# Probabilities of the sparse attention transposed by VectorE and moved by DMAs, instead of by TensorE through PSUM

## The chip, the cores and the metric

One core of one Trainium2 chip. The metric is the device time of one execution in microseconds (us); before and after are compared by the median of several runs. The rows shown come from one profiled execution.

## The reference, cut to what matters

A two-layer decoder trunk in float32: 512 tokens, model width 1024, batch 1. Layer 1 is retention with a gated output and a gated per-layer embedding. One projection then gives the keys and values of three attention branches, and a small MLP compresses one of them. Layer 2 is the sparse attention, in which 16 query heads of 4 groups attend to the compressed blocks, to selected blocks and to a window. With 512 tokens there are 8 selection blocks and up to 16 may be chosen, so that the selected branch, like the 512-token window, is plain causal attention here:

```python
s_s = jnp.einsum('bgrqd,bgqnkd->bgrqnk', q, ks).astype(jnp.float32) * scale
p_s = jnp.where(valid_s, jax.nn.softmax(jnp.where(valid_s, s_s, NEG), axis=(-2, -1)), 0.0)
o_s = jnp.einsum('bgrqnk,bgqnkd->bgrqd', p_s, vs.astype(jnp.float32))
...
return gates[..., 0:1] * o_c + gates[..., 1:2] * o_s + gates[..., 2:3] * o_w
```

The merged heads pass a SiLU gate and the output projection; a second gated embedding and a last RMSNorm end the kernel.

## The kernel before

Every float32 product is three matmuls (`mm3`, L355 of the profile) on operands split into a high and a low part: high by high, high by low, low by high. ScalarE makes the high part, VectorE subtracts it to get the low part (`split_psum`, L364 and L365).

**Weights** come as a stream of 128x1024 pieces (`Stream`). `load` (L143) issues the DMAs of pieces on SyncE's queue (SP) into four raw buffers, `mul` (L176, GpSimd) multiplies by the norm's gain, `high` (L190, ScalarE) and `low` (L205, VectorE) split. `W.tick` advances this by a step or two; the order of the pieces is written out in `order`, and a raw buffer is loaded anew once `low` has read it. The schedule is manual: each engine works in program order.

**The attention** has 4 groups `g` of 8 units `u`; a unit is one head `h` (`u // 2`) in one branch `b` (`u % 2`). A pass of the loop over `u` does:

- `scores` of the *next* unit: matmuls in three PSUM banks, mask (L937, L940), row maxima (L944) on VectorE, exponentials with row sums (L945) on ScalarE into `P[u % 2]`, of which there are two. For every second unit it also starts the compressed branch (`cmp_probs`, a generator advanced by `next(chain)`).
- up to four steps of `fillers` (`fill(0)` to `fill(2)`): halves of a gate or query projection (`g_proj`, `q_proj`), or pairs of tiles of the output projection (`pair_tiles`, whose sums VectorE adds at L1006).
- `scale_probs` of the next unit: the reciprocal (L954) and a product (L955) on VectorE, then four multiplications on GpSimd (L958).
- `probs_T` of the *present* unit: its lower triangle has ten 128x128 blocks. TensorE transposes them (L967) into the banks `pt`, eight in part 0 and two in part 1, and each bank is split into `tH` and `tL`.
- `values` of the present unit: the product of `tH`, `tL` with the values, which accumulates in bank `o` over the two branches of a head.

Between groups stand two `k_proj` (before the scores of the next group's unit 0) and four `v_proj` (after the group's last `values`). Group 3 has no projections after it. Before the attention lie the key and value projection (`v_proj` of group 0, from three pieces `kvb`) and the compression (`compress`), whose generators are interleaved with `c_proj` and the four `q_proj` of group 0; in it `block` adds a position vector (L783, VectorE) to gathered tokens and splits the sum (L785, L788).

## Time and profile before

| | |
|---|---|
| median of 3 runs | 1173.96 us (1173.95 to 1174.43) |
| the profiled execution: its own time | 1176.46 us |
| its span in the profile | 1174.7 us |
| granted TensorE clock, mean | 0.988 of full |
| busy: PE (matmul) | 1140.1 us, 97% |
| busy: DVE (VectorE) | 727.8 us, 62% |
| busy: ACT (ScalarE) | 490.8 us, 42% |
| busy: POOL (GpSimd) | 294.9 us, 25% |
| DMA moved | 101.90 MB, mean 87 GB/s |

PE is TensorE's matmul side, PEld its loading of weights, SPq the DMA issue on SyncE's queue. L and a number is a line of the kernel. A busy PE is not necessarily at its peak, since matmuls are pipelined and their ends are modelled: starts are the better measure. An idle time in brackets is that of the engine just before an instruction, with what ended it.

### The profile page before, as it was taken

The page shows a single profiled execution, that of the slowest core. Times are in us where ns is not written, and L with a number is a line of the kernel's source. Part 1 is how long each engine was busy: PE and PEld are TensorE (multiplying, and loading weights), DVE is VectorE, ACT ScalarE, POOL GpSimd, SP SyncE. Part 2 cuts the span into 40 slices and gives each one's busy share as a digit, 9 for nine tenths or more (in the row PEclk, how much of TensorE's full clock was granted, in tenths as well). Part 3 has the DMA queues.
Part 4 walks back from the last instruction along what each step waited for, and adds up shares of the span by engine and source line. Part 5 has one row for each costly group of instructions (what it writes and reads, how often), then busy time and mean ns, then how long its engine had stood idle before and what let it go on. Part 6 is the DMA issues. An engine that isn't in the chain of part 4 may idle for free. (4 is left out here: it accounts for less than half of the span.)

```text
span 1174.7 us, 15278 instructions
## 1 busy us (share of the span) xinstructions
PE 1140.1 (97%) x5806; PEld 970.0 (83%) x5806; DVE 727.8 (62%) x1242; ACT 490.8 (42%) x916; POOL 294.9 (25%) x341
## 2 busy tenths in 40 slices
PE   8999999999999999899699999999999999999997
PEld 7888888888888888888587888888898888887886
DVE  4746336544534556467857764778468774787555
ACT  6333233232323445345446443444344533444653
POOL 0212003002100222223435331454243431321012
PEclk9999999999999999999799999999999999999999
DMA  8422321322232131255512201221121211221211
GB/s 326 141 97 72 111 96 54 93 95 72 90 108 90 54 124 39 83 152 175 149 69 73 73 21 51 73 74 56 50 91 54 73 54 41 86 77 50 72 37 71
DMA packets 29593, 101.90 MB, mean 87 GB/s; under 512 B 3536, under 2 KB 3792, under 8 KB 29520
## 3 DMA queue, kind: packets, MB, share of 16 engines
q1 hardware_dynamic: 29088, 100.15, 26.2%
q8 instruction: 45, 0.74, 0.3%
q10 hardware_dynamic: 432, 0.79, 0.2%
q14 instruction: 28, 0.23, 0.1%
HBM read 98.83 MB, written 2.10 MB: 86 GB/s over the span
## 5 line engine op out<-in xcount | busy, mean ns | idle before, releaser
L355 PE MATMUL d<-arenaR 128*128 128x512 f32 (+2 forms) x2904 | 678.1, 386 | 10.4 <-DVE arenaF L1006 3.6
L355 PEld LDWEIGHTS d<-arenaR 128*128 128x128 f32 x2904 | 525.6, 189 | 113.9 <-DVE arenaF L1006 5.5
L355 PE MATMUL s<-arenaR 128*128 128x512 f32 (+8 forms) x1182 | 239.5, 353 | 0.2 <-DVE arenaR L829 0.2
L205 DVE TENSOR_TENSOR arenaR<-arenaF,arenaR 128x1024 fp32r<-128x1024 f32 (+1 forms) x142 | 194.1, 1386 | 66.1 <-ACT arenaR L190 66.0
L355 PEld LDWEIGHTS s<-arenaR 128*128 128x128 f32 x1182 | 200.3, 188 | 29.8 <-DVE arenaR L829 0.3
L190 ACT ACTIVATE arenaR<-arenaF 128x1024 fp32r<-128x1024 f32 (+1 forms) x142 | 145.8, 1048 | 104.4 <-PE s L355 68.4
L176 POOL TENSOR_TENSOR arenaF<-arenaF 128x512 f32<-128x512 f32 x108 | 137.0, 1291 | 126.2 <-DMA arenaF<-stream_dram 126.1
L355 PE MATMUL o<-arenaR 128*128 128x512 f32 (+3 forms) x744 | 133.4, 331 | 11.0 <-DVE arenaR L788 5.0
L355 PEld LDWEIGHTS o<-arenaR 128*128 128x128 f32 x744 | 119.1, 198 | 24.0 <-DVE arenaR L788 5.8
L958 POOL TENSOR_SCALAR arenaF<-arenaF 128x512 f32<-128x512 f32 (+3 forms) x128 | 66.8, 541 | 254.1 <-ACT arenaR L364 120.1
L945 ACT ACTIVATE arenaF<-s,arenaF 128x512 f32<-128x512 f32 (+3 forms) x128 | 67.6, 528 | 102.9 <-DVE arenaF L944 100.2
L365 DVE TENSOR_TENSOR arenaR<-pt,arenaR 128x512 fp32r<-128x512 f32 (+1 forms) x141 | 82.8, 617 | 35.5 <-ACT arenaR L364 33.8
L364 ACT ACTIVATE arenaR<-pt 128x512 fp32r<-128x512 f32 (+1 forms) x141 | 70.7, 540 | 80.0 <-PE pt L967 40.4
L371 POOL TENSOR_TENSOR arenaF<-arenaF 128x1 f32<-128x1 f32 (+1 forms) x25 | 14.2, 568 | 294.7 <-DVE arenaF L370 294.7
L944 DVE TENSOR_REDUCE arenaF<-s 128x1 f32<-128x512 f32 (+3 forms) x128 | 62.9, 491 | 22.2 <-ACT arenaF L945 18.9
L355 PE MATMUL pt<-arenaR 128*128 128x512 f32 (+1 forms) x384 | 75.9, 349 | 0.0
L355 PEld LDWEIGHTS pt<-arenaR 128*128 128x128 f32 x384 | 62.7, 188 | 9.4
L209 DVE SCALAR_TENSOR_TENSOR arenaR<-arenaF,arenaR 128x512 fp32r<-128x512 f32 x64 | 45.7, 762 | 35.0 <-PE pt L355 21.4
L194 ACT ACTIVATE arenaR<-arenaF 128x512 fp32r<-128x512 f32 x64 | 43.1, 721 | 46.6 <-issue 22.3
L967 PEld LDWEIGHTS pt<-arenaF 128*128 128x128 f32 x318 | 38.4, 141 | 12.1 <-DVE arenaR L365 4.5
L967 PE MATMUL pt<-arenaF 128*128 128x128 f32 x318 | 45.1, 273 | 3.2 <-DVE arenaR L365 3.2
L1006 DVE TENSOR_TENSOR arenaF<-arenaF,d 128x512 f32<-128x512 f32 x64 | 41.8, 682 | 7.0 <-PE d L355 6.7
(126 smaller groups left out, 692.6 us busy)
## 6 DMA issues: line engine op xcount, KB each, us to landing
arenaF<-stream_dram SPq DMA_DIRECT2D x174, 512.0 KB, 3.5
arenaF<-xT_dram SPq DMA_DIRECT2D x8, 256.0 KB, 5.0
arenaF<-x_dram SPq DMA_DIRECT2D x4, 512.0 KB, 8.3
out_dram<-arenaF SPq DMA_DIRECT2D x3, 512.0 KB, 2.6
arenaF<-cst_dram SPq DMA_DIRECT2D x4, 256.0 KB, 3.8
arenaF<-stream_dram ACTq DMA_DIRECT2D x2, 256.0 KB, 4.4
arenaF<-stream_dram SPq DMA_DIRECT2D x2, 256.0 KB, 6.0
arenaF<-cst_dram SPq DMA_DIRECT2D x1, 512.0 KB, 9.9
```

The lines of the kernel that those rows point to most:

```text
L176: self.nc.gpsimd.tensor_mul(r3[:, k], r3[:, k], g[:, k, None].to_broadcast([128, m // 2, w]))
L190: self.nc.scalar.activation(hi[:, :m * w], raw, AF.Copy)
L194: self.nc.scalar.activation(hi[:, c], raw[:, c], AF.Copy, scale=g[:, k:k + 1])
L205: self.nc.vector.tensor_sub(lo[:, :m * w], raw, hi[:, :m * w])
L209: self.nc.vector.scalar_tensor_tensor(lo[:, c], raw[:, c], g[:, k:k + 1], hi[:, c], op0=OP.mult, op1=OP.subtract)
L355: pe.matmul(o, a, b, start=start and i == 0, stop=stop and i == n - 1)
L364: act.activation(h, src, AF.Copy)
L365: dve.tensor_sub(l, src, h.bitcast(F32))
L944: dve.reduce_max(mx[:, i:i + 1], w, axis=mybir.AxisListType.X, negate=True)
L945: act.activation(Pu[:, PO[i]:PO[i] + n], w, AF.Exp, bias=mx[:, i:i + 1], accum_out=sm_[:, i:i + 1])
L958: pool.tensor_scalar(w, w, sm_[:, i:i + 1], 1.0, op0=OP.mult, op1=OP.mult)
L967: pe.transpose(p[:, f:f + 128], Pu[:, PO[i] + 128 * j:PO[i] + 128 * j + 128], ident)
```

## The change

- `probs_T` now serves the *next* unit. VectorE transposes 32x32 blocks inside each group of 32 partitions, four instructions that write `pt1`; then 16 DMAs on SyncE's queue, each of 32 partitions by 320 float32 (40 KB), move the squares between the groups of partitions into `pt2`. There is one `P`, one `pt1` and one `pt2`.
- `probs_split` (new) makes `tH` and `tL` of the present unit from `pt2` with one ScalarE and one VectorE instruction of 128x1280, both from SBUF. It stands after the scores of the next unit and ahead of `fill(0)` and `scale_probs`. `values` reads `tH` and `tL` in runs of 32 elements.
- `probs_T` stands after `fill(1)`, ahead of `W.tick`; that of the first unit before the loop.
- Beside it: `block` adds the position on GpSimd; the stream's order and the loop over `q_proj` put the last two compression pieces around the fourth `q_proj`; the first `v_proj` are cut in two (`v_sums`), so that the products with the first two of the three pieces of three token tiles come before those with the third.

```diff
     for n, dense in (("wk", [("kv", 0, 1024, 512 + 128 * g, 128) for g in range(4)]),
-                     ("wv", q(0)[:3])):
+                     ("wv", q(0))):
         o += [("w2", 0, 512, 0, 128)] if n == "wv" else []
         for i, d in enumerate(dense):
             o += [d] + [(n, 512 * (2 * i + e), 512, 0, 256) for e in (0, 1)]
-    o += [("wv", 512 * i, 512, 0, 256) for i in (6, 7)] + [q(0)[3]] + kk(0)
+    o += kk(0)
...
-    P = [V(fb + 4096 + 1280 * i, 1280) for i in range(2)]
+    g2 = [V(fb + o, 512) for o in (1664, 7680)]
+    P = V(fb, 1664)
+    pt1, pt2 = V(fb + 2176, 1280), V(fb + 3456, 1280)
...
-    def v_proj(g, t, p, bank="d", tick=True):
-        n = 256 if g else 304
-        o = psum(bank)[:, :n]
-        k0 = 0
+    def v_sums(t, o, p, k0):
         for q in p:
             m = q.h.shape[1]
             mm3(o, [(aH[:, t, k0 + k], aL[:, t, k0 + k], q.h[:, k], q.l[:, k])
                     for k in range(m)], k0 == 0, k0 + m == NK)
             k0 += m
+    def v_proj(g, t, p, bank="d", tick=True, o=None):
+        if o is None:
+            o = psum(bank)[:, :256]
+            v_sums(t, o, p, 0)
+        else:
+            v_sums(t, o, p[2:], 6)
...
-            dve.tensor_add(B[:, :, :, :31], src,
-                           pos[:, :, None, None].to_broadcast([128, 4, 4, 31]))
+            pool.tensor_add(B[:, :, :, :31], src,
+                            pos[:, :, None, None].to_broadcast([128, 4, 4, 31]))
...
-    v_proj(0, 0, p, "d", False)
-    v_proj(0, 1, p, "o", False)
+    o = [psum(bank)[:, :304] for bank in ("d", "o", "d", "s")]
+    v_sums(0, o[0], p[:2], 0)
+    v_sums(1, o[1], p[:2], 0)
     to_aT(3, hn[1])
-    v_proj(0, 2, p, "d", False)
+    v_sums(2, o[2], p[:2], 0)
+    v_proj(0, 0, p, tick=False, o=o[0])
+    v_proj(0, 1, p, tick=False, o=o[1])
     W.tick(1)
-    v_proj(0, 3, p, "s")
+    v_proj(0, 2, p, tick=False, o=o[2])
+    v_sums(3, o[3], p[:2], 0)
+    v_proj(0, 3, p, o=o[3])
...
-    for h in range(3):
+    for h in range(4):
         f = q_proj(0, h)
         next(f)
         if h < 2:
             next(comp)
+        if h == 3:
+            next(comp1)
         run(f)
         next(comp1)
-        next(comp1)
-    next(comp1)
-    next(comp1)
-    f = q_proj(0, 3)
-    next(f)
+        if h < 3:
+            next(comp1)
     act.activation(small[:, 250:251], half, AF.Exp)
-    next(comp1)
-    run(f)
...
-    PO = [896, 1024, 512, 0]
-    TO = [0, 512, 1024, 896]
+    PO = [0, 384, 768, 1152]
+    JB = [0, 128, 224, 288]
...
-                act.activation(Pu[:, PO[i]:PO[i] + n], w, AF.Exp, bias=mx[:, i:i + 1],
+                act.activation(P[:, PO[i]:PO[i] + n], w, AF.Exp, bias=mx[:, i:i + 1],
...
         for i in (3, 2, 0, 1):
-            w = Pu[:, PO[i]:PO[i] + 128 * i + 128]
+            w = P[:, PO[i]:PO[i] + 128 * i + 128]
             pool.tensor_scalar(w, w, sm_[:, i:i + 1], 1.0, op0=OP.mult, op1=OP.mult)
...
-    def probs_T(u, part, tag="pt"):
-        Pu = P[u % 2]
-        for j0, bank in (((0, (0,)), (1, (1, 3))), ((2, (2,)),))[part]:
-            p = psum(tag)
-            f = 0
-            for j in bank:
-                for i in range(j, NT):
-                    pe.transpose(p[:, f:f + 128], Pu[:, PO[i] + 128 * j:PO[i] + 128 * j + 128], ident)
-                    f += 128
-            c = slice(TO[j0], TO[j0] + f)
-            split_psum(tH[:, c], tL[:, c], p[:, :f])
+    def view(a, o, *ap):
+        return bass.AP(tensor=a.tensor, offset=a.offset + o, ap=[list(a.ap[0])] + [list(d) for d in ap])
+    def probs_T():
+        for j in range(NT):
+            dve.transpose(view(pt1, JB[j], (32, NT - j), (320, 4), (1, 32)),
+                          view(P, PO[j] + 128 * j, (384, NT - j), (32, 4), (1, 32)))
+        for a in range(4):
+            for b in range(4):
+                nc.sync.dma_start(pt2[32 * b:32 * b + 32, 320 * a:320 * a + 320],
+                                  pt1[32 * a:32 * a + 32, 320 * b:320 * b + 320])
+    def probs_split():
+        act.activation(tH, pt2, AF.Copy)
+        dve.tensor_sub(tL, pt2, tH.bitcast(F32))
     def values(g, u, o):
         h, b = divmod(u, 2)
         if b:
             pe.matmul(o, vcat[:96, 128 * g:128 * g + 128], pcat[h % 2][:96], start=False, stop=False)
         for j in (0, 1, 3, 2):
-            n = 512 - 128 * j
-            c = slice(TO[j], TO[j] + n)
             d = slice(128 * b, 128 * b + 128)
-            mm3(o[:, 128 * j:], [(v2H[:, j, d], v2L[:, j, d], tH[:, c], tL[:, c])], u % 2 == j == 0,
-                b == 1 and j == 2)
+            c = JB[j], (32, NT - j), (320, 4), (1, 32)
+            mm3(o[:, 128 * j:], [(v2H[:, j, d], v2L[:, j, d], view(tH, *c), view(tL, *c))],
+                u % 2 == j == 0, b == 1 and j == 2)
...
+    dve.tensor_scalar(bg, bg, 0.5, 0.5, op0=OP.mult, op1=OP.add)
     k_proj(0, 0)
     next(comp1)
-    w2p.done()
-    dve.tensor_scalar(bg, bg, 0.5, 0.5, op0=OP.mult, op1=OP.add)
     sums, chain = scores(0, 0)
     scale_probs(0, 0, sums)
+    next(comp1)
+    w2p.done()
+    probs_T()
     run(chain)
     k_proj(0, 1)
...
-            if g == u == 0:
-                fill(0)
             if nxt:
                 sums, chain = scores(*nxt)
-            if g or u:
-                fill(0)
+            probs_split()
+            fill(0)
             if sums is not None:
                 scale_probs(*nxt, sums)
-            probs_T(u, 0)
             next(chain, 0)
             fill(1)
-            probs_T(u, 1, "pt" if steps[1] else "d")
+            if sums is not None:
+                probs_T()
             W.tick(0 if last else 2)
```

## Rows read from the trace of the kernel before

**Rows 1.** The page, busy time, share of the span and instructions of each engine.

```profile
PE 1140.1 (97%) x5806; PEld 970.0 (83%) x5806; DVE 727.8 (62%) x1242; ACT 490.8 (42%) x916; POOL 294.9 (25%) x341
```

**Rows 2.** Windows: stretch and length, busy of each engine, granted clock, DMA share.

```profile
571.00:594.00 23.00, 14.39 (x58) 12.01 (x57) 16.15 (x11) 8.34 (x12) 17.01 (x15) 0.70 0.46 137
...
752.00:766.00 14.00, 13.59 (x72) 11.40 (x71) 11.90 (x28) 6.03 (x14) 2.06 (x4) 1.00 0.15 51
```

**Rows 3.** Timeline of PE in group 1: start, us, instruction, count.

```profile
743.04 1.03 PE L967 MATMUL pt<-arenaF 128*128 128x128 f32 x8
743.83 2.99 PE L355 MATMUL d<-arenaR 128*128 128x512 f32 x12
...
751.95 2.50 PE L355 MATMUL s<-arenaR 128*128 128x512 f32 x15
...
764.58 2.08 PE L355 MATMUL o<-arenaR 128*128 128x512 f32 x12
766.50 2.08 PE L355 MATMUL s<-arenaR 128*128 128x512 f32 x12
```

**Rows 4.** Timeline of PE between groups 1 and 2, and behind group 3.

```profile
838.72 11.07 PE L355 MATMUL d<-arenaR 128*128 128x512 f32 x48
849.63 2.50 PE L355 MATMUL s<-arenaR 128*128 128x512 f32 x15
...
860.70 3.05 PE L355 MATMUL d<-arenaR 128*128 128x256 f32 x24
...
872.22 2.10 PE L355 MATMUL s<-arenaR 128*128 128x512 f32 x12
...
1102.34 7.92 PE L355 MATMUL d<-arenaR 128*128 128x512 f32 x34
```

**Rows 5.** Timeline of ACT, DVE and POOL in the unit from 751.95.

```profile
756.75 0.19 ACT L945 ACTIVATION_READ_ACCUMULATOR arenaF<-s,arenaF 128x1 f32 x1
...
757.76 1.28 DVE L1006 TENSOR_TENSOR arenaF<-arenaF,d 128x512 f32<-128x512 f32 x2
...
758.96 0.17 DVE L954 RECIPROCAL arenaF<-arenaF 128x4 f32<-128x4 f32 x1
...
759.52 2.06 POOL L958 TENSOR_SCALAR arenaF<-arenaF 128x512 f32<-128x512 f32 x4 [10.06 <-DVE arenaF L955]
```

**Rows 6.** Groups: L190 and L944 (busy, mean ns), one line's durations (ns min/median/max).

```profile
L190 ACT ACTIVATE arenaR<-arenaF 128x1024 fp32r<-128x1024 f32 x138 | 142.6, 1055 | 104.4 <-PE s L355 68.4 <-PE d L355 14.9 <-PE pt L355 13.1
...
L944 DVE TENSOR_REDUCE arenaF<-s 128x1 f32<-128x512 f32 (+3 forms) x128 | 62.9, 491 | 22.2 <-ACT arenaF L945 18.9
...
L205 DVE TENSOR_TENSOR arenaR<-arenaF,arenaR x142: 681/1224/2166, 15.9 to 1093.1; 128x1024 fp32r<-128x1024 f32 x138, 128x912 fp32r<-128x912 f32 x2, 128x608 fp32r<-128x608 f32 x1, 128x512 fp32r<-128x512 f32 x1
```

**Rows 7.** SyncE's issues at the start, in time; then L143's durations (ns).

```profile
1.64 0.42 SPq L333 DMA_DIRECT2D arenaF<-stream_dram  x1
2.10 0.91 SPq L329 DMA_DIRECT2D arenaF<-xT_dram  x2
3.05 0.47 SPq L333 DMA_DIRECT2D arenaF<-stream_dram  x1
...
L143 SPq DMA_DIRECT2D arenaF<-stream_dram x174: 327/328/482, 8.5 to 1117.6; - x174
```

**Rows 8.** DMA issues: count, KB each, median us from issue to landing.

```profile
arenaF<-stream_dram SPq DMA_DIRECT2D x174, 512.0 KB, 3.5
...
out_dram<-arenaF SPq DMA_DIRECT2D x1, 256.0 KB, 2.3
...
arenaF<-gains_dram SPq DMA_DIRECT2D x1, 60.0 KB, 2.9
```

**Rows 9.** Timeline ahead of the attention: PE twice, POOL's first scaling.

```profile
475.30 0.96 PE L355 MATMUL d<-arenaR 128*128 128x304 f32 x5 [3.35 <-DVE arenaR L205]
...
576.31 0.79 PE L355 MATMUL o<-arenaR 128*128 128x256 f32 x2 [4.75 <-ACT arenaR L785]
...
609.17 2.06 POOL L958 TENSOR_SCALAR arenaF<-arenaF 128x512 f32<-128x512 f32 x4 [14.04 <-ACT arenaF L888]
```

More of the change, by code (lines that the diff above doesn't have):

```diff
@@ L688, in decoder @@
     kcH, kcL = R(rb + 14848, 128), R(rb + 14976, 128)
-    pc = [V(fb + 6656 + 512 * i, 128).rearrange("p (i n) -> p i n", i=4) for i in range(2)]
-    pc4 = [V(fb + 6784 + 512 * i, 384).rearrange("p (i r n) -> p i r n", i=4, r=3)
+    pc = [V(fb + 4736 + 512 * i, 128).rearrange("p (i n) -> p i n", i=4) for i in range(2)]
+    pc4 = [V(fb + 4864 + 512 * i, 384).rearrange("p (i r n) -> p i r n", i=4, r=3)
            for i in range(2)]
-    g2 = [V(fb + o, 512) for o in (2048, 7680)]
-    P = [V(fb + 4096 + 1280 * i, 1280) for i in range(2)]
+    g2 = [V(fb + o, 512) for o in (1664, 7680)]
+    P = V(fb, 1664)
+    pt1, pt2 = V(fb + 2176, 1280), V(fb + 3456, 1280)
     bk = [R(rb + o, 512) for o in (8192, 8704, 9216, 9728, 12800, 13312, 13824, 14336)]
@@ L952, in scale_probs @@
         h, b = divmod(u, 2)
-        Pu = P[u % 2]
         dve.reciprocal(sm_, sm_)
@@ L956, in scale_probs @@
         for i in (3, 2, 0, 1):
-            w = Pu[:, PO[i]:PO[i] + 128 * i + 128]
+            w = P[:, PO[i]:PO[i] + 128 * i + 128]
             pool.tensor_scalar(w, w, sm_[:, i:i + 1], 1.0, op0=OP.mult, op1=OP.mult)
-    def probs_T(u, part, tag="pt"):
-        Pu = P[u % 2]
-        for j0, bank in (((0, (0,)), (1, (1, 3))), ((2, (2,)),))[part]:
-            p = psum(tag)
-            f = 0
-            for j in bank:
-                for i in range(j, NT):
-                    pe.transpose(p[:, f:f + 128], Pu[:, PO[i] + 128 * j:PO[i] + 128 * j + 128], ident)
-                    f += 128
-            c = slice(TO[j0], TO[j0] + f)
-            split_psum(tH[:, c], tL[:, c], p[:, :f])
+    def view(a, o, *ap):
[11 more added lines that the diff above has]
+        dve.tensor_sub(tL, pt2, tH.bitcast(F32))
     def values(g, u, o):
```

## The prediction

> **What bounds the kernel now.** I read the page first. TensorE is busy for 97% of the span, VectorE for 62% [rows 1], so that work taken from TensorE should shorten the kernel if nothing else becomes late. I then read the timeline of PE through a unit and a border between groups: in group 1 one instruction follows the other, and a unit lasts 766.50 - 751.95 = 14.55 us [rows 3]. Third, the windows of that unit: VectorE is busy for 11.90 of its 14 us [rows 2]. It is much nearer to its limit here than its average says, and that is where the forecast is made. Last, the other engines in that unit [rows 5] and SyncE's issues [rows 7, 8].
>
> **What goes from TensorE.** Eight transposes move the next matmuls by 743.83 - 743.04 = 0.79 us [rows 3], 0.099 us each. Ten in each of 32 units are 320 x 0.099 = 32 us: the most that this part can give, since matmuls and splits stay the same in number of elements. The Trainium skill (TensorE: Matmul & The Clock Gate, Part 4) puts a transpose at about 275 ns in a kernel's context; by it 88 us would go. The trace decides for 32: these overlap, and the starts count.
>
> **What the change adds: a loop that TensorE is no part of.** Before, a unit's probabilities were scaled a whole unit ahead of their transposes. Now `probs_split` of unit u stands, in the program order of ScalarE and VectorE, ahead of the reciprocal of unit u+1; this leads to GpSimd's scaling, VectorE's transposes, the 16 DMAs and so to the split of u+1. Each step waits for the one before. Length, from the landing of the last DMA:
>
> - ScalarE's split, 128x1280: 1.25 times the 1.055 of 128x1024 [rows 6], 1.32 us.
> - VectorE's subtraction: 1.25 x 1.224 [rows 6], 1.53; at 2.85.
> - Evacuation of `fill(0)` queued between: none where it is the first half of a projection, otherwise up to the 1.28 of two `pair_tiles` sums [rows 5]. Mean, by my choice, 0.5; at 3.35.
> - Reciprocal to GpSimd's start: 759.52 - 758.96 = 0.56; four scalings 2.06 [rows 5]; at 5.97. VectorE waits in line, with at most `fill(1)`'s sums to do.
> - Four block transposes, which no row shows. The nearest have the same shapes and one tensor read: four row maxima, 4 x 0.491 = 1.97 [rows 6]. From half of that (1.0) to twice (3.9); I take 1.97; at 7.94.
> - Sixteen issues on SP: 15 pitches to the last. An issue lasts 0.328 us with 512 KB, and where issues follow at once, four starts span 3.05 - 1.64 = 1.41 us, 0.47 each [rows 7]. It is a price for each instruction, whatever its size. Bounds 0.35 (0.328 and a gap) and 0.47; I take 0.45, near the row of issues in a run: 6.75; at 14.7.
> - Landing of the last: 2.3 for 256 KB, 2.9 for 60 KB [rows 8]; a 40 KB move inside SBUF is not shown. I take 2.5; at 17.2.
> - Five hand-overs between engines, about 0.06 each: **17.5 us**. With all low ends 14.8; with all high ones 19.9.
>
> TensorE has about 14.55 - 0.99 = 13.6 us of work in that unit, so it waits some 4 us in each.
>
> A count of VectorE alone gives nearly the same. Its 11.90 busy us in the unit [rows 2] grow by 1.97, and in program order it must now also wait for ScalarE's split (1.3) and for the scaling (2.06 and hand-overs, less a sum of 0.7 or 1.3 that fits in): 16 to 17. Quicker DMAs alone would not bring the loop back to 13.6.
>
> **Where the loop applies.** Groups 0 to 2 have six steps each from the split of unit 0 to that of unit 6, group 3 seven to unit 7: 25 steps of 17.5. At a border between groups TensorE's projections hide the DMAs. From the split of unit 6: subtraction at 2.85, `values` 766.50 - 764.58 = 1.92 [rows 3], two `k_proj` 849.63 - 838.72 = 10.91 [rows 4], scores to the last row sum 756.75 + 0.19 - 751.95 = 5.0 [rows 3, 5], together 20.7. From there the same with `v_proj`, 872.22 - 860.70 = 11.52 [rows 4], in place of `k_proj`: 21.3. A border is 42.0. The first split: GpSimd's first scaling starts at 609.17 [rows 9]; 2.06 of scaling, 1.97 of transposes, 6.75 of issues, 2.5 to land and hand-overs end at 622.7. Behind the last split stand a subtraction and `values`, 5. The attention then ends at 622.7 + 25 x 17.5 + 3 x 42.0 + 5 = 1191.2 against 1102.34 now [rows 4]: **+89 us**. This is net of the 32.
>
> **The other edits** act where TensorE waits ahead of the attention. Near the compression's end VectorE is late: TensorE is busy for 14.4 of 23 us at a granted 0.70 of its clock, one wait lasting 4.75 us [rows 2, 9]. Moving `block`'s sums to GpSimd and putting the fourth `q_proj` between the last pieces fills part of the 8.6 idle us and keeps the clock up: from 4 to 13 us, I take 9. GpSimd's sums share its queue with `mul`, which is why I don't take all. The first `v_proj` wait 3.35 us for a third piece [rows 9]; the sums over two pieces fill this: 3.35, or some more with the clock; I take 4. Together **-13 us** (-7 to -17). The strided reads of `tH` I cost at nothing: TensorE has 4 spare us per unit; without that cover it would be 12 matmuls, 1.92 us at most again.
>
> **Sum.** 1176.46 of the profiled execution + 89 - 13 = 1252; its time stands 2.5 above the median of 1173.96, so **1250**.
>
> **Rivals.**
>
> *The DMAs stay hidden, and the kernel is faster.* For it: SyncE has few DMAs, and a unit of slack lies between transposes and `values`. With the loop below 13.6 us only the gains stay: 1174 - 32 - 13 = 1129. The point of decision is a loop of (1102.3 + 13 - 622.7 - 131) / 25 = 14.5 us, where the kernel keeps its time. Against it: even the low ends give 14.8, and VectorE's own count is above it. The Trainium skill (DMA: Bandwidth & Descriptors, Issuing engines are not separate DMA queues) says that the time to initiate a DMA is usually small relative to the DMA itself. By that the 6.75 us would nearly vanish. The rows of SP differ: an issue costs 0.33 to 0.47 us [rows 7], and sixteen come to more than one landing of 2.3 to 2.9 [rows 8]. Chance 0.09.
>
> *The weights come late too.* The stream's loads queue on SP behind the 16 issues, which wait for VectorE. A load freed in `W.tick` starts at about 15.2, lands 3.5 later [rows 8]; if GpSimd then multiplies it ahead of the next scaling, two pieces make that scaling some 2.3 us late, and the loop 19.8: 25 x 2.3 = 57 more, 1307. Against it: four raw buffers, of which seldom the newest is next. Chance 0.13.
>
> *The clock falls in each unit.* TensorE now idles for 4 us in a unit, and after waits of that kind the granted clock was 0.70 over 23 us [rows 2]. At that mean 13.6 us of work become 19.4, 1.9 more than the loop: 25 x 1.9 = 48 more, 1298. Against it: waits may be split up by its fillers. Chance 0.07.
>
> **How the numbers follow.** The forecast holds 0.69: a loop of 16.2 to 18.7, 1215 to 1285. A loop just at the decision point, and so a time within 0.2% (about what a measurement of this kernel can tell from no change), has 0.02. Faster is the first rival, 0.09; all else is slower, 0.89. The range reaches from the low ends of the unknown costs, 14.8 (622.7 + 25 x 14.8 + 131 - 1102.3 - 13 = +8; 1182) to the high ones, 19.9 (+136; 1310), which takes in the second and third rivals: 1185 to 1310.
>
> **What would show it.** In the profile after: PE's share well below 97%, with a wait of some us in each unit ahead of `values` or of a filler's bank; ScalarE waiting for DMAs in `probs_split`; VectorE waiting for L958's successor ahead of the transposes; starts of scores 16 to 19 us apart inside a group, near to before at the borders; 16 issues taking 5.5 to 7.5 us on SP; no half-speed stretch before the attention. The forecast fails if the issues take about 0.1 us each and the transposes under 1 us, or if ScalarE never waits for the split's DMAs.

## The result

The changed kernel takes 1369.8 us (median of 4 runs, 1368.1 to 1372.8) against 1174.2 for the kernel before on the same chip: a ratio of 1.1665, 95% interval 1.1638 to 1.1691. The forecast had the sign, and the loop as its cause, but not the size: 1250 was predicted, 1310 was the upper end of the range, and the slowdown is 2.6 times the one forecast.

The profiled execution of the changed kernel took 1368.33 us. Its page answers to [rows 1] with the busy line, and with the granted clock in tenths for 40 slices of the span:

```profile
PE 1160.4 (85%) x5486; PEld 973.2 (71%) x5486; DVE 753.1 (55%) x1290; ACT 484.8 (35%) x852; POOL 303.5 (22%) x357
...
PEclk9999999999999999988779979899788998878799
```

TensorE has 320 instructions fewer and is busy for longer, because its granted clock falls from the eighteenth slice on (580.8 to 614.9 us), in which the attention begins. No other engine has become the bound by its busy time: VectorE has gone from 62% to 55%. In this loop of waits the share of every engine falls.

Windows over the attention (stretch and length; PE, PEld, DVE, ACT, POOL busy; granted clock; DMA share; GB/s):

```profile
591.00:1261.00 670.00, 497.95 (x2329) 418.46 (x2330) 379.76 (x767) 209.31 (x429) 155.97 (x216) 0.85 0.24 74
```

The same work, from the first unit's mask on its scores to the last one's, took 481.3 us before (605.4 to 1086.7) and takes 669.5 now (591.3 to 1260.8): +188.2. It begins 14.1 us earlier, and what lies behind it is 17.7 us longer (88.0 to 105.7). 188.2 - 14.1 + 17.7 = 191.8, the difference of the two spans (1366.5 and 1174.7).

SyncE's timeline, answering to [rows 7], shows the loop as the starts of the sixteen issues (L978):

```profile
599.08 10.11 SPq L978 DMA_DIRECT2D arenaF<-arenaF  x16
...
738.03 11.04 SPq L978 DMA_DIRECT2D arenaF<-arenaF  x16
...
791.08 10.02 SPq L978 DMA_DIRECT2D arenaF<-arenaF  x16
...
874.91 10.02 SPq L978 DMA_DIRECT2D arenaF<-arenaF  x16
896.82 10.02 SPq L978 DMA_DIRECT2D arenaF<-arenaF  x16
916.18 10.04 SPq L978 DMA_DIRECT2D arenaF<-arenaF  x16
938.08 11.07 SPq L978 DMA_DIRECT2D arenaF<-arenaF  x16
970.32 10.82 SPq L978 DMA_DIRECT2D arenaF<-arenaF  x16
...
1097.09 10.03 SPq L978 DMA_DIRECT2D arenaF<-arenaF  x16
...
1150.40 10.03 SPq L978 DMA_DIRECT2D arenaF<-arenaF  x16
...
1273.00 10.02 SPq L978 DMA_DIRECT2D arenaF<-arenaF  x16
```

Sixteen issues take 10.0 us at the median (10.0 to 11.1), 0.63 each. The three borders between groups last 53.05, 54.14 and 53.31 us (738.03 to 791.08, 916.18 to 970.32, 1097.09 to 1150.40). The 25 steps inside groups share the rest: (1273.00 - 599.08 - 160.50) / 25 = **20.5 us** each. The prediction had 17.5 and 42.0. It cut from split to split, from that of unit 6 to that of the next group's unit 0 at a border; cut like this, a step is 20.46 and a border 54.1.

The step from 896.82, on ScalarE, VectorE and GpSimd (brackets: idle before, and what ended it):

```profile
908.33 1.28 ACT L982 ACTIVATE arenaR<-arenaF 128x1280 fp32r<-128x1280 f32 x1 [1.25 <-DMA arenaF<-arenaF]
909.64 1.49 DVE L983 TENSOR_TENSOR arenaR<-arenaF,arenaR 128x1280 fp32r<-128x1280 f32 x1 [3.22 <-ACT arenaR L982]
911.05 0.68 DVE L756 SCALAR_TENSOR_TENSOR arenaF<-arenaF,d 128x512 f32<-128x512 f32 x1
911.64 0.17 DVE L961 RECIPROCAL arenaF<-arenaF 128x4 f32<-128x4 f32 x1
912.19 2.05 POOL L965 TENSOR_SCALAR arenaF<-arenaF 128x512 f32<-128x512 f32 x4 [11.39 <-DVE arenaF L962]
914.27 1.84 DVE L974 STREAM_TRANSPOSE arenaF<-arenaF 128x512 f32<-128x512 f32 x4 [2.26 <-POOL arenaF L965]
```

From the first issue to the split 11.51 us pass (forecast 6.75 + 2.5 = 9.25, and a hand-over); the split takes 1.31, the subtraction 1.41 until the next starts, a filler's sum 0.59, the way to GpSimd 0.55, the scaling 2.08 and the transposes 1.91. The chain is the forecast's, link by link, and the link from the first issue to the split is longer. The step before, from 874.91, shows a second one: 21.91 us, since the sums of `fill(1)` stand ahead of the transposes on VectorE, and TensorE had made them only after waiting for a bank:

```profile
889.77 7.23 PE L355 MATMUL d<-arenaR 128*128 128x512 f32 x24 [7.66 <-DVE arenaF L1018]
...
892.74 0.69 DVE L1018 TENSOR_TENSOR arenaF<-arenaF,d 128x512 f32<-128x512 f32 x1 [2.13 <-PE d L355]
...
894.31 0.69 DVE L1018 TENSOR_TENSOR arenaF<-arenaF,d 128x512 f32<-128x512 f32 x1 [0.89 <-PE d L355]
894.92 1.84 DVE L974 STREAM_TRANSPOSE arenaF<-arenaF 128x512 f32<-128x512 f32 x4
```

GpSimd was done at 892.82 here; the transposes start at 894.92. TensorE idles 7.66 us for a bank that VectorE frees, and VectorE then waits 2.13 and 0.89 for TensorE, whose granted clock is 0.77 from 889.7 to 896.8.

A third link is longer in the step from 813.90: GpSimd multiplies weights that have just landed, and the scaling starts 2.75 us behind the reciprocal, where it was 0.55 above.

```profile
828.08 2.29 POOL L176 TENSOR_TENSOR arenaF<-arenaF 128x512 f32<-128x512 f32 x2 [18.99 <-DMA arenaF<-stream_dram]
828.39 0.17 DVE L961 RECIPROCAL arenaF<-arenaF 128x4 f32<-128x4 f32 x1
...
831.14 2.05 POOL L965 TENSOR_SCALAR arenaF<-arenaF 128x512 f32<-128x512 f32 x4
```

### The profile page after: what moved, and what is told of

Its sections match the earlier page's. It is cut to its first block, busy times and chain, and to the rows that moved or that the text cites. A ratio compares the mean times of both kernels' runs of the same rounds, so it can differ in the third digit from the quotient of the medians.

```text
span 1366.5 us, 15311 instructions
## 1 busy us (share of the span) xinstructions
PE 1160.4 (85%) x5486; PEld 973.2 (71%) x5486; DVE 753.1 (55%) x1290; ACT 484.8 (35%) x852; POOL 303.5 (22%) x357
## 5 line engine op out<-in xcount | busy, mean ns | idle before, releaser
L355 PE MATMUL d<-arenaR 128*128 128x512 f32 (+2 forms) x2904 | 701.7, 397 | 130.6 <-DVE arenaF L1018 56.2
L355 PEld LDWEIGHTS d<-arenaR 128*128 128x128 f32 x2904 | 548.0, 196 | 246.8 <-DVE arenaF L1018 59.4
L205 DVE TENSOR_TENSOR arenaR<-arenaF,arenaR 128x1024 fp32r<-128x1024 f32 (+1 forms) x142 | 180.2, 1287 | 65.7 <-ACT arenaR L190 65.4
L190 ACT ACTIVATE arenaR<-arenaF 128x1024 fp32r<-128x1024 f32 (+1 forms) x142 | 146.0, 1046 | 138.4 <-PE s L355 68.4
L355 PE MATMUL o<-arenaR 128*128 128x512 f32 (+3 forms) x744 | 149.2, 353 | 47.4 <-ACT arenaR L982 33.3
L355 PEld LDWEIGHTS o<-arenaR 128*128 128x128 f32 x744 | 129.2, 212 | 69.0 <-ACT arenaR L982 35.6
L176 POOL TENSOR_TENSOR arenaF<-arenaF 128x512 f32<-128x512 f32 x108 | 123.0, 1160 | 181.4 <-DMA arenaF<-stream_dram 176.9
L965 POOL TENSOR_SCALAR arenaF<-arenaF 128x512 f32<-128x512 f32 (+3 forms) x128 | 65.6, 531 | 345.9 <-DVE arenaF L962 290.6
L983 DVE TENSOR_TENSOR arenaR<-arenaF,arenaR 128x1280 fp32r<-128x1280 f32 x32 | 47.8, 1492 | 127.8 <-ACT arenaR L982 127.8
L974 DVE STREAM_TRANSPOSE arenaF<-arenaF 128x512 f32<-128x512 f32 (+3 forms) x128 | 57.9, 490 | 48.1 <-POOL arenaF L965 47.0
L355 PE MATMUL pt<-arenaR 128*128 128x512 f32 (+1 forms) x384 | 77.4, 355 | 0.0
L982 ACT ACTIVATE arenaR<-arenaF 128x1280 fp32r<-128x1280 f32 x32 | 40.6, 1269 | 94.5 <-DMA arenaF<-arenaF 94.4
L997 ACT ACTIVATE arenaR<-arenaF 128x512 fp32r<-128x512 f32 x16 | 10.1, 632 | 153.3 <-DVE arenaF L996 153.3
L194 ACT ACTIVATE arenaR<-arenaF 128x512 fp32r<-128x512 f32 x64 | 43.1, 720 | 46.6 <-issue 22.3
```

Of the source, the lines that this page charges most:

```text
L176: self.nc.gpsimd.tensor_mul(r3[:, k], r3[:, k], g[:, k, None].to_broadcast([128, m // 2, w]))
L190: self.nc.scalar.activation(hi[:, :m * w], raw, AF.Copy)
L194: self.nc.scalar.activation(hi[:, c], raw[:, c], AF.Copy, scale=g[:, k:k + 1])
L205: self.nc.vector.tensor_sub(lo[:, :m * w], raw, hi[:, :m * w])
L355: pe.matmul(o, a, b, start=start and i == 0, stop=stop and i == n - 1)
L965: pool.tensor_scalar(w, w, sm_[:, i:i + 1], 1.0, op0=OP.mult, op1=OP.mult)
```

## The experiments

Four theories came up in turn. A: the sixteen moves are the whole excess, and without them TensorE sets the unit again. B: VectorE's own line holds a unit at 16 to 17 us without any move. C: what holds it is the place of the split, ahead of the fillers. D: the order in which VectorE must run its work, together with the fillers' two PSUM banks. All ratios are against the kernel before, measured beside each (1173.1 to 1174.5 us). Eight runs leave out moves or transposes, or move the blocks to other places (e1, e2, e6, e9, e10, e13, e14, e16); they don't compute the whole result and tell of time only.

### The moves away, the moves halved, the other edits alone, the scaling first

**e1_no_moves** leaves the sixteen moves out, and the split reads the transposed blocks where they are:

```
-        for a in range(4):
-            for b in range(4):
-                nc.sync.dma_start(pt2[...], pt1[...])
-        act.activation(tH, pt2, AF.Copy)
-        dve.tensor_sub(tL, pt2, ...)
+        act.activation(tH, pt1, AF.Copy)
+        dve.tensor_sub(tL, pt1, ...)
```

> Leaves out the 16 DMAs of a unit; the split reads the block transposes unmoved, so the probabilities are not fully transposed. Theory A (a loop through split, scaling, transposes and the DMAs sets a unit, and the DMAs are 12 of its 20.4 us): the loop falls to about 8.5 us, below TensorE's own 13, and only the gains of the change are left: 1174 - 32 - 14 = about 1130 us. Theory B (VectorE's program order, with its waits for the split and the scaling, is a bound of 16 to 17 us of its own, as the prediction counted): 25 steps stay some 3.5 us above TensorE's, about 1215 us.

Measured: 1243.2 us, ratio 1.0581 (1.0559 to 1.0603). The moves cost 126.6 of the 195.6 us. Theory A falls: 69 us remain.

**e2_eight_moves** issues eight moves of twice the size, the same bytes:

```
-            for b in range(4):
-                nc.sync.dma_start(pt2[32 * b:32 * b + 32, 320 * a:320 * a + 320], pt1[...])
+            for b in range(2):
+                nc.sync.dma_start(pt2[32 * a:32 * a + 32, 640 * b:640 * b + 640], pt1[...])
```

> Eight DMAs of 32 partitions by 640 elements (80 KB) in place of 16 of 320 (40 KB): the same bytes, half the instructions; the squares land in other places than the product needs. Theory A with a price per issue (0.63 us): the loop loses 8 x 0.63 = 5.0 us, 25 steps and the borders 125 to 140 us: about 1235 us. Rival, a price by bytes (the moves are slow because of what they carry): about 1370 us as before the edit.

Measured: 1264.8, ratio 1.0770 (1.0752 to 1.0788): 105 us less, for the same bytes. SyncE's timeline has

```profile
816.52 4.95 SPq L978 DMA_DIRECT2D arenaF<-arenaF  x8
```

and the page's list of DMA issues (KB each, us to landing)

```profile
arenaF<-arenaF SPq DMA_DIRECT2D x256, 80.0 KB, 2.1
```

Eight issues take 4.95 us, again 0.62 each, and 80 KB land in 2.1 us against 1.9 for 40 KB. For these moves the price belongs to the instruction, not to the bytes, as the prediction said; its amount was wrong.

**e3_other_edits** is the kernel before with the change's other edits alone (order of the stream, `v_sums`, `block`'s sums on GpSimd, the order of `q_proj`):

```
+    v_sums(0, o[0], p[:2], 0)
...
+            pool.tensor_add(B[:, :, :, :31], src, ...)
...
+    for h in range(4):
+        f = q_proj(0, h)
```

> The attention of the kernel before (transposes on TensorE, its own layout and order) with the other edits of the change alone: sums of the compression on GpSimd, order of the last pieces, first value projection cut in two. Theory A: these gave the 14 us by which the first DMA of the changed kernel came earlier than forecast: 1174 - 14 = about 1160 us. Rival (the earlier start comes from the attention's own prologue, and the edits give nothing): 1174 us.

Measured, in six runs: 1169.52, ratio 0.9965 (0.9952 to 0.9977). Its first mask comes 14.9 us earlier (590.5 against 605.4), as forecast, but its attention then takes 487.9 us in place of 481.3, and the kernel gains only 5 in all. It is the fastest kernel here that computes the whole result.

**e4_scale_first** puts the next unit's scaling ahead of the split:

```
-            probs_split()
-            fill(0)
             if sums is not None:
                 scale_probs(*nxt, sums)
+            probs_split()
+            fill(0)
```

> The changed kernel with scale_probs of the next unit ahead of probs_split of the present one, nothing else: reciprocal and scaling no longer wait for the DMAs. Theory A: the loop loses reciprocal, hand-over and scaling, 2.6 to 3.3 us of 20.4; 25 steps give 65 to 85 us: about 1295 us. Rival (the DMAs queue on SyncE and it is SyncE's own rate, 10 us of issues with loads behind, that sets the unit; or VectorE's program order): no change beyond 10 us, about 1365 us.

Measured: 1345.2, ratio 1.1458 (1.1441 to 1.1474). Taking the scaling off the path from landing to issue gives 25 us, a third of what was expected: the transposes that follow still stand behind the split and `fill(0)` on VectorE.

### The place of the split, and another way to move

**e5_split_late** moves the split behind `fill(1)`, right ahead of the transposes; **e6_no_moves_late** does this without the moves:

```
-            probs_split()
             fill(0)
...
             fill(1)
+            probs_split()
             if sums is not None:
                 probs_T()
```

> The changed kernel with probs_split behind fill(1), just ahead of the next unit's probs_T, instead of ahead of fill(0); all 16 DMAs kept. Theory C (two limits: the loop through the DMAs, and the fillers' PSUM sums that queue behind the split on ScalarE and VectorE and leave TensorE without a free bank): the fillers' sums and the scaling leave the wait, the loop is split 1.3 + 1.5, transposes 1.84, issues 10.0, landing 1.9, hand-overs: 16.9 in place of 20.4; 25 steps give about 90 us: 1280 us. Rival (what counts is only the scaling in the loop, as the run with the scaling first showed it): about 1345 us.

> The run without the DMAs (they are left out, so the probabilities are not fully transposed), with probs_split behind fill(1) as well. Theory C: nothing holds the fillers' banks any more, TensorE runs through, and the time falls from 1243 to 1135 to 1170 us, near TensorE's and VectorE's own 13 us in a unit. Rival (VectorE's sum of work and forced waits is 16 us in whatever order): it stays at 1220 to 1243 us.

Measured: 1299.2, ratio 1.1065 (1.1048 to 1.1082), and 1241.8, ratio 1.0574 (1.0558 to 1.0589). With the moves the late split saves 70.6 us; without them it saves nothing (1243.2 to 1241.8). Theory C falls: with two banks, the place matters because the moves land late.

**e7_bounce5** sends the blocks through DRAM, one DMA out and four back, with the late split:

```
+        dr = dpool.tile([128, 1280], F32, name="dr")
+        nc.sync.dma_start(dr, pt1)
+        for b in range(4):
+            nc.sync.dma_start(pt2[32 * b:32 * b + 32].rearrange("p (a n) -> p a n", a=4),
+                              bass.AP(tensor=dr.tensor, offset=dr.offset + 320 * b,
+                                      ap=[[1280, 32], [40960, 4], [1, 320]]))
```

> As the run with the split behind fill(1), but the squares move through DRAM: one DMA of 640 KB out and four of 160 KB back, 5 instructions in place of 16 and correct probabilities. By the rows (landing of 512 KB 2.7 to 3.6 us, issues 0.63): about 3.5 + 4 x 0.63 + 2.5 = 8.5 us in place of 11.9. Theory C: the loop falls to 13.5 us: 1165 to 1195 us. Rival (DRAM's round trip costs as much as the issues saved): about the time of the run with 16 DMAs, 1280 us.

Measured: 1250.1, ratio 1.0651 (1.0625 to 1.0677): 49 us less than e5, and 8 from e6, which moves nothing. SyncE's issues in one unit:

```profile
819.21 0.33 SPq L978 DMA_DIRECT2D dr<-arenaF  x1
822.19 1.75 SPq L980 DMA_DIRECT2D arenaF<-dr  x4
```

and the landings on the page:

```profile
dr<-arenaF SPq DMA_DIRECT2D x32, 640.0 KB, 2.9
arenaF<-dr SPq DMA_DIRECT2D x128, 160.0 KB, 3.2
```

Two landings one after the other, and five issues, are over in about 8 us (2.98 + 1.75 + 3.2 from 819.21), where the sixteen need 11.4 to their last landing (median of 32). Of the 76 us that are left above the kernel before, 67 are in e6 too, which moves nothing.

**e8_T_first** gives the transposed probabilities a second buffer and puts the split behind the next unit's transposes (sixteen moves):

```
-            probs_split()
             fill(0)
...
-                probs_T()
+                probs_T(nxt[1])
+            probs_split(u)
```

> Two buffers for the moved probabilities, and probs_T of the next unit behind fill(1) and ahead of probs_split of the present one; all 16 DMAs. The transposes no longer wait for the split, so that the loop spans two passes: transposes 1.84, DMAs 11.9, split 2.8, values 1.9, then scores, exponentials and scaling of the unit after next 9.5: 28 us for two units, 14 each. Theory C: about 1190 us. Rival (SyncE's 10 us of issues and the loads behind them set the unit): 1270 us or more, as with the split behind fill(1).

Measured: 1294.2, ratio 1.1032 (1.0983 to 1.1080). Now TensorE's `values` wait for the subtraction, 66 us in 28 places. The time lies where the rival had it, but not for its reason: SyncE itself waits 217.5 us in 30 places for VectorE's transposes, so its issues and loads don't set the unit.

### What is left without moves

**e9_banks** (on e6) lets every second `pair_tile` take its PSUM bank from the tag `pt`, which the change leaves nearly idle:

```
-        o = psum("d")
+        o = psum(("d", "pt")[t % 2])
```

**e10_no_blocks** (on e6) makes the four transposes of a unit one short one that still reads all four scaled blocks:

```
-        for j in range(NT):
-            dve.transpose(view(pt1, JB[j], (32, NT - j), (320, 4), (1, 32)), view(P, ...))
+        dve.transpose(view(pt1, JB[0], (32, NT), (1, 32)), view(P, PO[0], (384, NT), (1, 32)))
```

> Edit on e6 (no moves between partitions, split behind the second fillers; 1241.77 us): every second pair sum takes its PSUM bank from the tag pt, which the change left nearly idle, so the fillers have four banks instead of two. Nothing else moves. As in e6, the probabilities are not fully transposed. Theory D, part 1 (what is left above before without the moves is VectorE's program order: transposes, waits for POOL's scaling, the split, the weights' low parts and the next mask stand one behind the other, and more banks do not shorten that line): 1225 to 1242. Theory D, part 2 (the fillers' two d banks are the tie: TensorE waits for d about 1 to 3 us a unit on the pair sums, and with a bank more it runs on): 1180 to 1205.

> Edit on e6: the four VectorE transposes of a unit (1.84 us) become one of 128 elements a partition that still reads a piece of every scaled block, so the wait for POOL's scaling stays; the rest of the transposed buffer is filled once. The probabilities are not transposed at all. VectorE's line loses about 1.55 us in each of 32 units, 50 us in all. Theory D, part 1 (VectorE's program order sets the unit): 1175 to 1200, with some of it as granted clock coming back. Rival (the tie is the d banks, or TensorE at its lower clock): at least 1225.

Measured: 1220.0, ratio 1.0394 (1.0377 to 1.0411), and 1214.1, ratio 1.0352 (1.0289 to 1.0416). Each takes a part, 22 and 28 us, and each less than its own half of theory D had promised. The four runs of e10 lie between 1207.6 and 1223.4, so that its 28 is the less certain.

**e11_bounce_pool** (on e7) moves the split's subtraction to GpSimd and takes e9's banks:

```
-        dve.tensor_sub(tL, pt2, tH.bitcast(F32))
+        pool.tensor_sub(tL, pt2, tH.bitcast(F32))
```

> Edit on e7 (moves as one DMA to DRAM and four back, split behind the second fillers; 1250.13 us): the split's subtraction (1.49 us on VectorE) goes to GpSimd, which is busy 22% of the span, and pair sums take every second bank from the tag pt. It computes the whole result. If VectorE's line sets the unit, 32 x 1.49 = 48 us come off: 1195 to 1215, perhaps less with the banks. If GpSimd's slower subtraction only moves the wait to TensorE's values (GpSimd stands between the casts, the scaling and this in program order): 1235 to 1260. It would have to reach 1174 to equal the kernel before.

Measured: 1263.6, ratio 1.0754 (1.0721 to 1.0787), slower than e7. GpSimd needs 2.9 us for what took VectorE 1.49 (mean of its group, in ns), and TensorE's `values` wait for it, 66 us in 30 places:

```profile
L986 POOL TENSOR_TENSOR arenaR<-arenaF,arenaR 128x1280 fp32r<-128x1280 f32 x32 | 93.0, 2905 | 18.8 <-ACT arenaR L985 17.5 <-POOL arenaF L966 1.2
```

**e12_two_queues** (on the changed kernel) issues eight of the sixteen from ScalarE:

```
-                nc.sync.dma_start(pt2[...], pt1[...])
+                (nc.sync, nc.scalar)[b % 2].dma_start(pt2[...], pt1[...])
```

> Edit on the changed kernel (1369.8 us): of the sixteen moves of a unit, eight are issued by ScalarE's queue and eight by SP's; sizes and targets stay. If the 0.63 us from one issue to the next belongs to the issuing queue, each does its eight in 5 us side by side, and the time falls by nearly what eight moves of twice the size gave (1264.8): 1265 to 1295, with ScalarE now waiting for the transposes and paying eight issues. Rival (the 0.63 us is a rate shared by all queues, or landing): sixteen still take 10 us and it stays at 1355 to 1385, or gets worse since ScalarE is held.

Measured: 1430.6, ratio 1.2193 (1.2170 to 1.2217), slower by 61. The timeline of both queues and of ScalarE's next work:

```profile
833.39 4.96 SPq L978 DMA_DIRECT2D arenaF<-arenaF  x8
833.41 5.26 ACTq L978 DMA_DIRECT2D arenaF<-arenaF  x8
...
838.72 2.00 ACT L190 ACTIVATE arenaR<-arenaF 128x1024 fp32r<-128x1024 f32 x2 [14.28 <-DMA arenaF<-arenaF]
```

The queues do what was expected, they issue side by side, and sixteen are out in 5.3 us; the time of 1265 to 1295 expected from it was missed. ScalarE stands in program order in front of its eight DMAs until VectorE's transposes are done, and then issues for 5.26 us; the weights' casts (L190) start only then, and the idle time ahead of them, ended by its own DMAs, is 14.28 us.

### The three parts together, and the wait for GpSimd

**e13_early_banks** is e1 with e9's banks. **e14_early_banks_nb** is that with e10's one short transpose. **e15_bounce_banks** is e7 with e9's banks and the split moved up, behind the scaling:

```
             if sums is not None:
                 scale_probs(*nxt, sums)
+            probs_split()
             next(chain, 0)
             fill(1)
-            probs_split()
```

> Edit on e1 (no moves between partitions, split where the change has it; 1243.2 us): pair sums take every second PSUM bank from the tag pt, as in e9 (1219.98, where TensorE's remaining waits were 50 us for the late split). The probabilities are not fully transposed. Theory D, in three parts (VectorE's line, the two d banks, the place of the split): with the banks free and the split ahead of the fillers, TensorE no longer waits for either: 1180 to 1205. Rival (an early split only moves the wait from the values to the fillers' gates, which keep the d banks, or to the scaling): 1215 to 1240.

> Edit on e13: the four VectorE transposes of a unit become one of 128 elements a partition, as in e10. The probabilities are not transposed at all. If the parts add up (e10 took 28 us off e6, and e9 took 22), this comes within 15 us of the kernel with the change's other edits alone (1169.5): 1165 to 1185. If something else is left, such as the single buffer of probabilities, which lets the next unit's exponentials start only behind the transposes: 1190 or more.

> Edit on e7 (moves as one DMA to DRAM and four back, 1250.13): pair sums take every second bank from the tag pt, the subtraction stays on VectorE, and the split stands behind the scaling of the next unit and ahead of the second fillers. It computes the whole result. Theory D: 1195 to 1230, the early split's part being limited by when the data lands, some 8 us after the transposes. Rival (the landing binds at the earlier place): 1250 or more. It would have to reach 1174 to equal the kernel before.

Measured: 1227.7, ratio 1.0461 (1.0437 to 1.0485); 1201.5, ratio 1.0239 (1.0219 to 1.0259); 1230.4, ratio 1.0482 (1.0460 to 1.0505). The parts don't add up to the whole: e14 is 32 us above the other edits alone. The row of its one transpose says what is left, in the idle time ahead of it:

```profile
L973 DVE STREAM_TRANSPOSE arenaF<-arenaF 128x128 f32<-128x128 f32 x32 | 10.0, 312 | 51.8 <-POOL arenaF L965 50.8 <-POOL arenaF L1026 1.0
```

VectorE stands still for 50.8 us, 1.6 in each unit, until GpSimd has scaled.

**e16_no_wait** (on e14) lets this transpose read constants; **e17_descending** (on e15) keeps it all, but lets scaling and transposes both go through the blocks from the last to the first:

```
-                      view(P, PO[0], (384, NT), (1, 32)))
+                      view(gn, 0, (32, NT), (1, 32)))
```

```
-        for i in (3, 2, 0, 1):
+        for i in (3, 2, 1, 0):
             w = P[...]
...
-        for j in range(NT):
+        for j in (3, 2, 1, 0):
             dve.transpose(...)
```

> Edit on e14 (no moves, split early, four banks, one short block transpose a unit; 1201.53 us): the short transpose reads constants in place of the scaled probabilities, so VectorE no longer stands still for GpSimd's scaling (in e14 it waits 49.1 us for it in 30 places). Nothing of the probabilities is transposed. Theory: this wait is the last part of the difference to the other edits alone (1169.5), so 1165 to 1180. Rival (the remainder is the split's single wide form and the order, the wait for GpSimd only fills time that VectorE has): 1193 to 1203.

> Edit on e15 (one move to DRAM and four back, four banks; 1230.39 us): GpSimd scales the query blocks in the order 3, 2, 1, 0 and VectorE transposes key blocks in the order 3, 2, 1, 0, so that a transpose starts once the scaled blocks it reads are there, and not once all four are. It computes the whole result. In e15 VectorE waits 36.5 us for the scaling. If a transposition may start ahead of the last scaling: 1200 to 1220. Rival (the instruction waits for all four all the same, or the wait only moves to the next place): 1225 to 1235.

Measured: 1155.1, ratio 0.9827 (0.9798 to 0.9856), and 1219.9, ratio 1.0393 (1.0371 to 1.0416). The wait alone is worth 46.4 us: nearly the whole of the idle time in the row above. Windows of e14 and of e16 over the attention:

```profile
591.00:1110.00 519.00, 470.32 (x2333) 399.04 (x2334) 351.41 (x673) 206.19 (x428) 177.96 (x217) 0.94 0.17 57
```

```profile
591.00:1070.00 479.00, 456.30 (x2347) 389.62 (x2345) 340.64 (x681) 211.75 (x437) 205.33 (x217) 0.98 0.19 62
```

TensorE's work is the same in both. It takes 14.0 us less in e16, at a granted clock of 0.98 in place of 0.94. GpSimd's scaling, beside which VectorE no longer stands still, takes 0.89 us for one of its instructions in e16 against 0.53 in e14 (L965, mean of 128). In e17 the wait shrinks from 36.5 to 10.3 us, but the time only by 10.5: VectorE's waits for ScalarE ahead of the two subtractions (L366, L986) grew from 57 to 62 us in the meantime. What took the rest was not traced further.

## Why the prediction was right, and where not

**What bounds the change: right.** TensorE waits because a loop outside it sets the unit. The loop runs where the prediction put it, ScalarE waits for DMAs ahead of the split, and the shares fall.

**The step that failed is the price of the sixteen issues,** "15 pitches to the last ... Bounds 0.35 ... and 0.47; I take 0.45 ... 6.75". They take 10.0 us, 0.63 each, outside the bounds. This is the largest of three errors; the two others, what VectorE's order adds and the length of the borders, follow below. The rows that the price rested on were of loads from DRAM [rows 7]; the moves go from 32 partitions to 32 others, and no row of before showed one. From first issue to split it was 11.74 against 9.25 on the mean of the 25 steps, +2.5: the 15 pitches 9.62 in place of 6.75, the landing 2.12 in place of 2.5. e2 and e1 confirm its weight, 105 us for eight issues fewer and 127 for all. Eight issues a unit are 8 x 0.63 = 5.0 us, 161 in 32 units, of which e2 won 105; where the rest went was not traced.

The price alone does not make the miss. Between e2 and the changed kernel the way from first issue to last landing differs by 4.9 us (6.5 and 11.4, medians) and the time by 105; by that rate 2.5 us are 54, an estimate, and the forecast's price would have given some 1316, still above the 1310.

The Trainium skill (DMA: Bandwidth & Descriptors, Issuing engines are not separate DMA queues) calls the time to initiate a DMA usually small relative to the DMA itself, and issuing from several engines a saving of this time alone. The trace differs on the first for these small moves: one issue takes 0.63 us, a third of its landing of 1.9, and sixteen in a row 10.0. On the second e12 agrees as to the issues, 5.3 us in place of 10.0; its kernel became slower all the same.

**The second part is VectorE's program order.** The 0.5 us for `fill(0)` were right (0.48 on the mean). But the forecast let `fill(1)`'s sums fit into the wait for GpSimd and gave what outlasts it nothing. In 8 of the 25 steps TensorE makes them late and the transposes start 1.1 to 3.1 us behind the end of the scaling, 0.8 on the mean. Third, GpSimd multiplies weights ahead of the scaling in 5 of the 25, as in the rows from 828.08: 0.8 to 2.2 us, 0.3 on the mean. The other links are together 0.5 shorter than forecast. In all, 25 x (20.5 - 17.5) = 75 us.

**The borders: +11.5 each,** 42.0 forecast against a mean of 53.5. The rival of late weights, given 0.13, acts here above all; inside the groups it comes to 7.4 us of the 57 that it named. Five loads wait on SP until the sixteen issues from 938.08 are out:

```profile
949.26 10.32 SPq L143 DMA_DIRECT2D arenaF<-stream_dram  x5
...
953.27 2.04 POOL L176 TENSOR_TENSOR arenaF<-arenaF 128x512 f32<-128x512 f32 x2 [17.14 <-DMA arenaF<-stream_dram]
...
955.35 1.06 ACT L190 ACTIVATE arenaR<-arenaF 128x1024 fp32r<-128x1024 f32 x1 [8.86 <-POOL arenaF L176]
...
956.31 0.36 ACT L364 ACTIVATE arenaR<-d 128x256 fp32r<-128x256 f32 x1
...
959.10 0.29 DVE L948 TENSOR_TENSOR s<-s,masks 128x128 f32<-128x128 f32 x1
```

GpSimd waits 17.14 us for the load; behind it come ScalarE's cast, `v_proj`'s split and only then the mask on scores that TensorE had begun at 950.71. The forecast counted the border by TensorE's work, and this chain isn't TensorE's. From the split at 930.81 to the one at 963.08 it is 32.3 against 21.3 forecast: scores to last row sum take 12.5 in place of 5.0, and `v_proj` 15.2 in place of 11.5, at a granted clock of 0.89 and with waits. Without the moves (e1) the borders last 47.9 to 49.1, and before the change 47.3 to 47.5 (from scaling to scaling), so about 6 of the 11.5 are there without any move: the count of 42.0 was short by itself.

**Ends.** The first split comes at 610.69; 622.7 less 13 was forecast. That it is right to a microsecond is in part luck: the first issue comes 1.2 us earlier than forecast, and the DMAs take 2.4 longer. The last split comes at 1284.58 in place of 1173: 75 + 3 x 11.5 + 1 = 110.5 of those 111.6 are the terms above. From there to the end it is 81.9 us against 77.4 (1174.7 - 1102.34 + 5). That closes the account: 111.6 + 4.5 = 116.1 between the 1252 of the prediction's sum and the profiled 1368.3.

**Right in size.** Four transposes take 1.84 us (1.97 forecast), the scaling 2.05, the ScalarE split 1.27, the subtraction 1.49. The strided reads of `tH`, taken at nothing, cost nothing at full clock: the 12 matmuls from 912.29 move the next by 1.93 us, against 1.92. The alternative count, VectorE with its waits at 16 to 17 us a unit, is borne out by the runs without moves: inside the groups the transposes start 16.8 us apart in e1 and 16.0 in e13 (means of 25 steps). Over the attention e1 takes 82.0 us more than before (563.3 against 481.3).

**The range** was added up too short at its upper end: the links with the high values that the list gives make 20.1 us, not 19.9, and so 1315, not 1310. The measured time lies outside either way.

**The other edits, -13: right in mechanism, too large in worth.** The start is 14 to 15 us earlier, but alone they give 5.0 (e3); 6.6 come back in the attention.

**The transposes on TensorE, -32: too large for what came back.** With nearly everything that replaces them taken away (e16), the kernel is 14.4 us faster than the other edits alone, four banks included. In the attention TensorE is busy for 20.5 us less (476.8 in e3, 456.3 in e16) but idle for 11.5 more (11.2 and 22.7). e16 keeps the change's order, its one `P` and its wide splits, so that 14.4 is what was left with these, not a bound for every order.

```profile
L967 PE MATMUL pt<-arenaF 128*128 128x128 f32 x318 | 45.1, 273 | 3.2 <-DVE arenaR L365 3.2
```

The Trainium skill (TensorE: Matmul & The Clock Gate, Part 4) has about 275 ns for a transpose in one kernel's context. The trace of before agrees for a single one, 273 ns in the row above, but in a run they start 0.099 us apart [rows 3]. So the 88 us, an estimate from the page's figure, are further off than the 32.

**The whole sum, by medians,** from the other edits alone (1169.5): transposes off TensorE, with the change's order, splits and four banks, -14.4 (e16); VectorE's wait for GpSimd's scaling, +46.4 (e14); VectorE's block transposes but for 0.3 us, +26.2 (e13); two banks in place of four, +15.5 (e1); sixteen moves, +126.6: 1369.8. The terms depend on the order in which they are taken: from e6 the transposes were worth 28 and the banks 22. In e10, e14 and e16 most of what `values` reads is zero; whether that moves the granted clock was not tried, which leaves -14.4 and +26.2 open to it, but not the +46.4, where both runs have it.

**The clock: a rival at 0.07, and in fact a part of every case.** In the attention the granted clock was 1.00 before, 0.98 in e16, 0.92 in e1 and 0.85 after the change. TensorE's busy time there rose from 472.0 (windows of before, 605 to 1087) to 498.0 although 32 us of work had gone. How much of the time this costs by itself, beyond what the waits cost, no run here separates.

**Left open.** No version with the transposes on VectorE came under the kernel before; e17 is the nearest with the whole result, 1219.9. It differs from e16 by 64.8 us: block transposes, what is left of the wait, the place of the split and the way through DRAM, which no run takes apart. The one pair that differs by the way through DRAM alone is e6 and e7, 8.4 us (1241.8 and 1250.1). That the five loads at a border wait for the issues is read from the trace; no run moved them.

## What to carry to other kernels

An engine at 60% of the span may be at 85% of the stretch that matters; then what it does there goes to the time in good part: of 49 us less work (32 x 1.53) 26 to 28 came back, and of 50.8 us of standing still for another engine, 1.6 a unit, 46. Count a set of DMAs by its instructions, with a price from rows of the same kind of move, and if none is there let the range say so: here 0.63 us in place of 0.45 was the largest single error. And before moving work off the busiest engine, ask what it can give at most: here 32 us stood in the rows, and 14 came back with nearly all that replaced it taken away.

## What had not been expected of the hardware

- An issue of a 40 KB move between partitions takes 0.63 us on SP and 0.66 on ScalarE's queue, and of 80 KB 0.62, against 0.33 to 0.47 for loads of 512 KB and 0.44 (1.75 / 4) for 160 KB from DRAM to SBUF. Partitions, rows and source differ between these; which of them sets the price was not tried.
- Five DMAs through DRAM (640 KB out, four of 160 KB back) are done in about 8 us, sooner than sixteen moves inside SBUF in 11.4, and cost the kernel 49 us less (e7 against e5).
- GpSimd took 2.9 us for a 128x1280 subtraction that VectorE does in 1.49 (e11).
- GpSimd's scaling went from 0.53 to 0.89 us an instruction when VectorE stopped standing still beside it (e14, e16).
